# A list scheduler that issues products on part of the array in runs of one shape

## The chip, the core and the metric

The kernel runs on one core of one Trainium2 chip, in one launch. The metric is the time on the device in microseconds, median of the runs. TensorE (PE in the profile) multiplies; VectorE (DVE), ScalarE (ACT) and GpSimd (POOL) do the rest; the DMAs are issued from SyncE's queue (SP). PEld is the weight load that comes with each matmul.

## What is computed

Two transformer blocks of two layers each, on 256 tokens of width 1024, in float32. Cut to the parts that the change touches:

```python
def first_block(x, c, ...):                      # DEPTH = 2 layers
    for l in range(DEPTH):
        mod = c_act @ ada_w[l] + ada_b[l]        # adaLN vector, 6 x 1024
        h = rms_norm(x, norm1_g[l]) * (1.0 + sc1) + sh1
        proj = h @ w_in[l]
        y_a = diff_attention(...)                # 4 heads, two softmaxes of width 64 each
        y_b = gated_deltanet(...)                # chunks of 64 tokens, both directions
        merged = g_a * (y_a @ w_branch_a[l]) + g_b * (y_b @ w_branch_b[l])
        x = x + gt1 * (merged @ w_out[l])
        h = rms_norm(x, norm2_g[l]) * (1.0 + sc2) + sh2
        x = x + gt2 * (jnp.square(jax.nn.relu(h @ w_mlp1[l])) @ w_mlp2[l])

def diff_attention(...):
    s = jnp.einsum('bhtqd,bhtkd->bhtqk', qi, k) * scale      # contraction over 64
    p = jax.nn.softmax(s, axis=-1)
    a = p[:, :, 0] - lam * p[:, :, 1]

def gated_delta_rule_chunked(q, k, v, g, beta):  # per head and chunk of 64
    L = jnp.where(strict, jnp.einsum('bhncd,bhnmd->bhncm', kb, k) * decay, 0.0)
    T = lax.linalg.triangular_solve(eye + L, eye, ...)       # 64 x 64
    def step(state, inp):                                    # the scan over chunks
        v_new = u_i - w_i @ state
        o_i = qd_i @ state + qk_i @ v_new
        state = state * gl_i + kd_i.T @ v_new
```

The second block has two layers too: an attention stage of three kinds of heads, then 16 experts with 32 slots each, whose weights are 192 units of 1 MB a layer.

## The kernel before

Nothing in the kernel is issued as it is written. The program is recorded first: every operation becomes an `Op` with its engine, its operands and a cost in ns (`Plan.add`, `Plan.cost`), and a list schedule (`Plan.schedule`, line 465) then makes the order in which all engines' instructions are issued. Each engine takes, among the operations whose operands are there at the earliest time at which it could go on, the one with the largest `key`, the longest way to the end. `Plan.keys` works the keys out by a schedule that runs backwards. Operations get slots of tiles as they are scheduled; `can` says from when an operation's tiles have slots. `flush` (line 579) then issues all in the order of the plan's start times, which is why nearly every row of the profile has line 596.

What PE is given is of two kinds. **Full products** use 128 rows and 128 columns of the array: the projections (`dense`, lines 780 to 813), whose fp32 operands are split into two fp32r parts, three products for one, mostly 256 columns wide, and transposes. **Partial products** use part of the array. In block 1 the main ones are: the scores of the differential attention (`first` in `diffattn`, line 1493: 64 rows, in the upper and the lower half of the array by turns), the products of 64x64 blocks that complete the triangular inverse (`prod` in `deltanet`, line 1321: two corners of the array), and the products of the scan (lines 1399, 1403 and 1417: 128 rows by 64 columns, and 64 by 128). Further ones are 32 columns wide: column sums (line 1083), adaLN (lines 923 and 949), and the gates' weights of the recurrence (line 1116); the k k^T blocks (line 1216) have 128 by 64. In block 2 the attention has some of both kinds, and the experts' products are 128x32 (lines 2079 and 2095) and 32x128 (line 2102). Partial products that lie in different parts of the array and in one bank are recorded as one operation of two or four products (`add`, line 378).

The order on PE has one rule beyond the keys. `small` (line 518) counts up by the cost of each partial product whose contraction or whose width is 64 or less, and down by three times the cost of each other product; while it stands above `SMALL`, 1000 ns, other products are preferred (lines 533 and 534). Otherwise keys alone decide, so a partial product that has the larger key and a full one that has the next can stand in turns.

In block 1 `deltanet`, with the recurrence's chain of products and of steps on DVE, ACT and GpSimd, is woven with `fill` (line 1626): the attention, the gates' products and the first branch product. Weights come as units of 1 MB through a stream (`Stream`, line 740): ACT and DVE or GpSimd split each. In layer 0 the stream also brings 40 units of adaLN weights, with sums on DVE (line 942) and GpSimd (line 935).

Scratch tiles of 256 columns are of the kind `w1`: 8 in one pool and `W1X` = 6 more, in block 1 alone (line 1678).

Of the kernel before, what the change touches and what calls it, by code (L numbers as in the profile page):

```python
# [20 lines left out]
NEG = -1e30  # L21
# [8 lines left out]
W1X, NT = 6, 10  # L30


# ---------------------------------------------------------------- host layout
def _units(w, n=2):
    """[K, N] -> [N/(128 n), 128 (k in chunk), n, K/128, 128]: lhsT units of n column chunks."""
    k, c = w.shape
    a = w.reshape(k // 128, 128, c // (128 * n), n, 128).transpose(2, 1, 3, 0, 4)
    return np.ascontiguousarray(a).reshape(c // (128 * n), 128, -1)


def _rows(w, kc):
    """[K, N] -> [K/(128 kc), 128, kc, N]: rhs units of kc row chunks."""
    k, c = w.shape
    a = w.reshape(k // (128 * kc), kc, 128, c).transpose(0, 2, 1, 3)
    return np.ascontiguousarray(a).reshape(k // (128 * kc), 128, -1)


def _cols(v):
    """[n*128] -> [128, n]"""
# [14 lines left out]
def _shape_consts():  # L64
    """constants of the program, packed by the time that they are needed: c0 always, c1 and c2 per block"""
# [71 lines left out]
def _bias(rpb):  # L137
    """[4, 15, 31] -> [4, 128 (q in tile), 2 * 256]: bias of q over k, NEG outside q's window"""
# [92 lines left out]
def _rows_n(w, n):  # L231
    """[1024, N] -> [N/n, 128, 8, n]"""
# [5 lines left out]
# ---------------------------------------------------------------- order of issue  # L238


class Ref:
    """an access pattern of a tile that gets its place when its operations are issued"""
# [28 lines left out]

class Tile:
# [3 lines left out]
class Op:  # L276
    __slots__ = ("eng", "calls", "group", "outs", "dur", "dma", "deps", "succ", "tiles", "start", "end", "key", "what", "small")


class Plan:  # L280
    """Operations are recorded in program order and issued in the order of a list schedule: each engine takes,
    among the operations whose operands are there, the one with the longest way to the end. Costs and latencies
    are the guide's, in ns; they depend on shapes alone. A tile's slot is given out ahead of program order only if
    program order could still go on from there. Products that fill half of the array or less are not issued in long
    rows while others are ready: the array's clock falls when it is used little."""
# [4 lines left out]
    SMALL = 1000.0  # L290
# [12 lines left out]
    # -------------------------------------------------------- recording  # L303
# [22 lines left out]
    def box(r):  # L326
        """(what, partitions from, to, columns from, to)"""
# [37 lines left out]
    def add(self, eng, name, fn, args, kw):  # L365
# [4 lines left out]
        if eng == "P" and self.cols(ins[0]) < 128 and name == "matmul":  # L370
            p = self.ops[-1]
            rng = outs[0].ap.ap[0][1], outs[0].ap.offset // outs[0].ap.ap[0][0]
            if p.group and p.outs[0].t is outs[0].t and rng not in p.group:
                p.group.append(rng)
                self.access(p, n - 1, ins, outs)
                p.calls.append((fn, args, kw))
# [7 lines left out]
        if eng == "P":  # L384
            k, n_ = ins[0].shape[0], self.cols(ins[1])
            o.small = name == "matmul" and min(k, n_) <= 64
        o.eng, o.calls, o.dma, o.deps, o.succ, o.start, o.tiles = eng, [(fn, args, kw)], None, set(), [], None, []
# [38 lines left out]
    # -------------------------------------------------------- scheduling  # L426
# [3 lines left out]
    def keys(self, n0):  # L430
        """time to the end by a list schedule that runs backwards, in which every engine is single"""
# [33 lines left out]
    def schedule(self, slots):  # L465
        """slots: per kind of tile, the time at which each slot gets free"""
# [24 lines left out]
        def fit(e, t, dur):  # L491
            """the first time from t on at which engine e is idle for dur"""
# [8 lines left out]
        def can(i, t):  # L501
            """the earliest time from t on at which operation i's tiles have slots"""
# [15 lines left out]
        order, small = [], 0  # L518
        while len(order) < n - n0:
# [3 lines left out]
            for e, q in ready.items():  # L523
# [6 lines left out]
                if c:  # L530
                    t0 = min(c)[0] + 1
                    c = [(-ops[i].key, t, i) for t, i in c if t <= t0]
                    if e == "P" and small > self.SMALL:
                        c = [z for z in c if not ops[z[2]].small] or c
# [6 lines left out]
            if o.eng == "P":  # L541
                small = max(0.0, small + (o.dur if o.small else -3 * o.dur))
# [36 lines left out]
    def flush(self, place, slots, issue):  # L579
        """schedules what has been recorded, into what waits and has gaps; place(kind, slot): the slot's memory"""  # L580
# [8 lines left out]
        for i, place in self.waiting:  # L589
# [5 lines left out]
            for fn, args, kw in o.calls:  # L595
                self.tc.keep_in_program_order(fn(*map(real, args), **{k: real(v) for k, v in kw.items()}))  # L596
# [3 lines left out]
# ---------------------------------------------------------------- program  # L600


def _build(nc, tc, A, out):
# [10 lines left out]
    def sigm(o, x):  # L614
        """o = sigmoid(x) = exp(-log(1 + exp(-x))): the functions of a single table set"""
# [27 lines left out]
    with es:  # L643
# [10 lines left out]
        def issue(blocks, own, acc, quarters=(), last=False):  # L654
            """blocks: kind -> the blocks that its slots lie in; own: kind -> the pools of its further slots;
            acc: PSUM banks for accumulators; quarters: pools of the blocks whose quarters are tiles for themselves"""
# [66 lines left out]
        class FM:  # L723
            """feature-major activations: chunk pairs of 2 x 256 tokens, one tile each"""
# [15 lines left out]
        class Stream:  # L740
            """weights in the order of their use: loads run ahead, the split into two fp32r halves a little less"""
# [15 lines left out]
            def split(self, key):  # L757
                """loads and splits the next unit, if it isn't there yet"""
# [16 lines left out]
            def take(self, key):  # L775
                """an item that is used as it is"""
# [3 lines left out]
        def dense(st, key, n, kc, xhi, xlo, evac, fresh=False):  # L780
            """feature-major [128, 256] outputs, two per bank; a half of a unit at a time.
            n units of n * 2048 / (128 kc) column chunks; fresh: x comes in chunk by chunk"""
# [1359 lines left out]
```

## Time and profile before

| | us |
|---|---|
| median of 3 runs | 2407.26 (2403.64 to 2407.43) |
| span of the profiled execution | 2408.3 |
| PE busy | 1984.8 (82%) |
| DVE busy | 1159.4 (48%) |
| ACT busy | 786.9 (33%) |
| GpSimd busy | 465.6 (19%) |

The profile gives no time of its own for the profiled execution beside its span; the span is 1.0 us over the median of the runs. Block 1 takes about the first 1215 us, its two layers about 690 and 525; the first layer of block 2 ends about 1816 us. The views read are the busy times of chosen stretches, with the granted clock of PE (1.00 is 2.4 GHz, 0.50 is 1.2 GHz) and the DMA engines' share; the list of who waited for whom in a stretch; the timeline of PE, in which equal instructions that follow each other are one row; and the list of groups of instructions. A matmul's duration in the timeline overlaps with its neighbours', so what one costs is read from the starts. A product of fp32 operands stands as two instructions, one of fp32r as one.

### The profile page before, as it was taken

To read this page: it belongs to the slowest core of one execution; us is meant where nothing else is said; L and a number is where in the kernel's file an instruction comes from. 1 tells how busy PE (TensorE), PEld (TensorE's weight loads), DVE (VectorE), ACT (ScalarE), POOL (GpSimd) and SP (SyncE) were. 2 spreads that over 40 slices of the span, in tenths; PEclk is the share of its full clock that TensorE was granted. 3 is DMA by queue.
4 is the path that set the end of the run, shared out by engine and by line. 5 is a ranking of instruction groups with operands and counts; after the bars stand their busy time and mean duration, and the time that the engine had idled before them with its cause. 6 is when DMAs were issued, how large, how long until landed. Compare 5 with 4: busy or idle time off the path is not lost. (4 is left out here: it accounts for less than half of the span.)

```text
span 2408.3 us, 38449 instructions
## 1 busy us (share of the span) xinstructions
PE 1984.8 (82%) x16200; PEld 1437.7 (60%) x16200; DVE 1159.4 (48%) x1908; ACT 786.9 (33%) x1508; POOL 465.6 (19%) x278
## 2 busy tenths in 40 slices
PE   8688987778989999999999887666769988666665
PEld 5677777777987777999986542222237644222222
DVE  5998478999789623775557410000006731000001
ACT  4363343433457323654456210000015521000001
POOL 1555354455133312000020210000002111000000
PEclk7897898788999768999999888887779988877777
DMA  8354224566633310645544699999995579999997
GB/s 315 124 188 128 105 106 158 210 229 254 237 121 132 116 36 18 247 158 178 203 153 167 274 420 420 421 421 420 421 420 212 209 281 420 420 421 420 420 421 313
DMA packets 108253, 622.36 MB, mean 258 GB/s; under 512 B 27184, under 2 KB 28464, under 8 KB 34992
## 3 DMA queue, kind: packets, MB, share of 16 engines
q1 hardware_dynamic: 108080, 619.90, 65.4%
q8 instruction: 127, 2.08, 0.3%
q14 instruction: 46, 0.38, 0.0%
HBM read 617.24 MB, written 2.62 MB: 257 GB/s over the span
## 5 line engine op out<-in xcount | busy, mean ns | idle before, releaser
L596 PE MATMUL ps<-quarter,block 128*128 128x256 f32 (+1 forms) x5760 | 868.4, 304 | 72.5 <-DVE quarter L596 23.6
L596 PEld LDWEIGHTS ps<-quarter,block 128*128 128x128 f32 x5760 | 786.2, 205 | 114.9 <-issue 28.2
L596 PE MATMUL ps<-block,block 128*32 128x256 f32 (+4 forms) x5204 | 546.5, 431 | 137.9 <-DMA block<-in_w_up_dram 95.1
L596 PEld LDWEIGHTS ps<-block,block 128*32 128x32 f32 (+2 forms) x5204 | 274.4, 136 | 354.7 <-DMA block<-in_w_up_dram 159.3
L596 DVE TENSOR_TENSOR block<-block,block 128x1024 fp32r<-128x1024 f32 (+2 forms) x262 | 364.7, 1398 | 130.6 <-PE ps L596 73.1
L596 ACT ACTIVATE block<-block 128x1024 fp32r<-128x1024 f32 (+2 forms) x312 | 319.1, 1028 | 321.9 <-PE ps L596 292.8
L596 ACT ACTIVATE w<-ps 128x256 f32<-128x256 f32 (+1 forms) x138 | 52.3, 382 | 819.0 <-PE ps L596 818.9
L596 DVE TENSOR_TENSOR w<-w,ps 128x256 f32<-128x256 f32 x64 | 26.9, 421 | 544.3 <-ACT w L596 537.8
L596 POOL TENSOR_TENSOR block<-block,block 128x1024 fp32r<-128x1024 f32 x46 | 117.0, 2551 | 794.3 <-ACT block L596 387.8
L596 PE MATMUL ps<-block,w 128*32 128x256 f32 x2048 | 176.0, 500 | 25.8 <-ACT w L596 13.3
L596 PE MATMUL ps<-quarter,quarter 64*64 64x64 f32 (+6 forms) x1312 | 166.8, 304 | 6.9 <-DVE quarter L596 6.9
L596 PEld LDWEIGHTS ps<-block,w 128*32 128x32 f32 x2048 | 76.9, 142 | 116.2 <-issue 49.8
L596 PEld LDWEIGHTS ps<-quarter,quarter 64*64 64x64 f32 (+3 forms) x1312 | 113.2, 177 | 53.2 <-issue 20.0
L596 ACT ACTIVATE quarter<-quarter 128x512 f32<-128x512 f32 (+2 forms) x188 | 116.2, 628 | 85.0 <-DVE quarter L596 82.5
L596 ACT ACTIVATE quarter<-ps 128x512 f32<-128x512 f32 (+1 forms) x136 | 79.5, 592 | 151.2 <-PE ps L596 133.8
L596 DVE SCALAR_TENSOR_TENSOR w<-block,cT,w 128x256 f32<-128x256 f32 x140 | 126.5, 903 | 2.2
L596 DVE TENSOR_SCALAR w<-c,slot 128x256 f32<-128x256 f32 x32 | 12.5, 411 | 234.9 <-PE ps L596 234.8
L596 PE MATMUL ps<-w,w 32*128 32x256 f32 x512 | 106.7, 418 | 15.4 <-ACT w L596 15.1
L596 POOL TENSOR_TENSOR block<-block,cT 128x2048 f32<-128x2048 f32 x20 | 76.5, 3825 | 136.8 <-DVE w L596 41.0
L596 PEld LDWEIGHTS ps<-w,w 32*128 32x128 f32 x512 | 55.5, 185 | 69.2 <-issue 35.4
L596 DVE TENSOR_TENSOR quarter<-quarter,ps 128x512 f32<-128x512 f32 (+1 forms) x80 | 49.0, 629 | 84.7 <-PE ps L596 80.0
L596 POOL TENSOR_TENSOR block<-block 128x1024 f32<-128x1024 f32 (+1 forms) x40 | 85.2, 2131 | 2.4
(169 smaller groups left out, 1604.8 us busy)
## 6 DMA issues: line engine op xcount, KB each, us to landing
block<-in_w_gate_dram SPq DMA_DIRECT2D x144, 1024.0 KB, 19.8
block<-in_w_up_dram SPq DMA_DIRECT2D x128, 1024.0 KB, 19.8
block<-in_w_down_dram SPq DMA_DIRECT2D x128, 1024.0 KB, 19.8
block<-in_w_m_dram SPq DMA_DIRECT2D x64, 1024.0 KB, 4.8
block<-in_ada_dram SPq DMA_DIRECT2D x40, 1024.0 KB, 6.1
block<-in_w_dn_dram SPq DMA_DIRECT2D x16, 1024.0 KB, 4.8
block<-in_w_o_dram SPq DMA_DIRECT2D x16, 1024.0 KB, 7.0
block<-in_w_in_dram SPq DMA_DIRECT2D x12, 1024.0 KB, 12.1
```

What stands on the lines that cost most here:

```text
L596: self.tc.keep_in_program_order(fn(*map(real, args), **{k: real(v) for k, v in kw.items()}))
```

## The change

The rule with `small` goes. In its place, once PE has been given a partial product, it is given further operations of the same shape (rows and columns of the array) as long as one is among the candidates of that moment; a transpose counts as full. After a full product keys alone decide, as before. And whenever the shape changes while PE has been idle for less than `CHANGE` = 300 ns, the operation's start in the plan is set to 300 ns after the end of the one before. `W1X` falls from 6 to 3, so block 1 has 11 scratch tiles of 256 columns in place of 14. The further lines keep, for each operation, the source line that it comes from, and add no instruction. Cut to this:

```diff
-W1X, NT = 6, 10
+W1X, NT = 3, 10
...
-    SMALL = 1000.0
+    CHANGE = 300.0
...
-            o.small = name == "matmul" and min(k, n_) <= 64
+            o.shape = (k, self.cols(ins[0])) if name == "matmul" else (128, 128)
...
-        order, small = [], 0
+        order, shape = [], (128, 128)
...
-                    if e == "P" and small > self.SMALL:
-                        c = [z for z in c if not ops[z[2]].small] or c
+                    if e == "P" and shape != (128, 128):
+                        c = [z for z in c if ops[z[2]].shape == shape] or c
...
             if o.eng == "P":
-                small = max(0.0, small + (o.dur if o.small else -3 * o.dur))
+                if o.shape != shape and at["P"] > t - self.CHANGE:
+                    t = at["P"] + self.CHANGE
+                shape = o.shape
...
-            for fn, args, kw in o.calls:
-                self.tc.keep_in_program_order(fn(*map(real, args), **{k: real(v) for k, v in kw.items()}))
+            for fn, args, kw, n in o.calls:
+                self.tc.keep_in_program_order(
+                    call_at(n)(fn, tuple(map(real, args)), {k: real(v) for k, v in kw.items()}))
```

What this does to the order is seen at two places on PE. The first is in layer 1 of block 1, where the scores of a head begin. Before (all rows have line 596; `quarter` and `block` are tiles, `ps` a bank of PSUM, and 128x256 the output; rows that read a `block` are full products of the gates, the others are scores):

```order
L596 MATMUL ps_63<-quarter_1_5970,block_491 128x256
L596 MATMUL ps_91<-quarter_0_7254,quarter_3_7121 128x256
L596 MATMUL ps_63<-quarter_0_5976,block_491 128x256
L596 MATMUL ps_91<-quarter_3_7264,quarter_3_7121 128x256
L596 MATMUL ps_63<-quarter_1_5970,block_491 128x256
L596 MATMUL ps_91<-quarter_0_7254,quarter_0_7126 128x256
```

After (L838 is a full product, L1518 a score):

```order
L838 MATMUL ps_63<-quarter_1_6009,block_486 128x256
L1518 MATMUL ps_83<-quarter_0_7253,quarter_0_7167 128x256
L1518 MATMUL ps_91<-quarter_0_7253,quarter_0_7167 128x256
L1518 MATMUL ps_83<-quarter_2_7267,quarter_0_7167 128x256
L1518 MATMUL ps_91<-quarter_2_7267,quarter_0_7167 128x256
L1518 MATMUL ps_83<-quarter_0_7253,quarter_1_7176 128x256
L1518 MATMUL ps_91<-quarter_0_7253,quarter_1_7176 128x256
```

Scores and full products stood in turns, twelve times for a head; now 24 scores follow each other, those of the upper and the lower half of the array by turns.

The second is a little further on, in the 64x64 products of the triangular inverse (each row two products). Before:

```order
L596 MATMUL ps_79<-quarter_2_7431,quarter_0_6877 64x64 x2
L596 MATMUL ps_71<-quarter_3_5990,block_518 128x256
L596 MATMUL ps_79<-quarter_2_7431,quarter_0_6877 64x64 x2
L596 MATMUL ps_91<-quarter_0_7439,quarter_3_6888 64x64 x2
L596 MATMUL ps_67<-quarter_1_6006,block_491 128x256
```

After (L1346 is a 64x64 product, L836 a full one):

```order
L1346 MATMUL ps_83<-quarter_0_7336,quarter_2_6800 64x64 x2
L836 MATMUL ps_63<-quarter_1_5979,block_478 128x256
L1346 MATMUL ps_83<-quarter_0_7336,quarter_2_6800 64x64 x2
L1346 MATMUL ps_79<-quarter_1_7410,quarter_2_7345 64x64 x2
L1346 MATMUL ps_83<-quarter_0_7336,quarter_2_6800 64x64 x2
L1346 MATMUL ps_79<-quarter_1_7410,quarter_2_7345 64x64 x2
```

Between two full products stand eight such rows now, sixteen products, where one or two rows stood for most of the way. In between, one full product still comes: it has the largest key once no product of the shape is left.

## Rows read from the trace of the kernel before

**Rows 1.** Busy us and instructions by stretch, granted clock, DMA share; the first row names columns.

```profile
core 0: us, PE busy (x) PEld busy (x) DVE busy (x) ACT busy (x) POOL busy (x), PEclk, DMA share, GB/s
200.00:360.00 160.00, 143.09 (x1077) 113.57 (x1075) 107.92 (x171) 61.12 (x135) 70.52 (x50) 0.85 0.31 109
360.00:690.00 330.00, 270.75 (x2008) 257.96 (x2009) 291.42 (x353) 129.68 (x194) 131.64 (x57) 0.89 0.56 211
...
800.00:960.00 160.00, 154.95 (x918) 114.80 (x919) 61.61 (x125) 48.34 (x96) 31.16 (x31) 0.72 0.14 43
960.00:1215.00 255.00, 250.95 (x2045) 248.31 (x2044) 167.39 (x228) 132.02 (x196) 10.94 (x6) 0.99 0.55 197
1215.00:1340.00 125.00, 121.71 (x712) 95.84 (x711) 88.48 (x197) 76.73 (x184) 21.79 (x14) 1.00 0.44 162
1340.00:1816.00 476.00, 340.72 (x3525) 153.36 (x3524) 43.68 (x114) 52.55 (x127) 26.94 (x18) 0.81 0.98 407
...
1950.00:2383.00 433.00, 313.77 (x3332) 136.13 (x3330) 24.08 (x59) 35.39 (x85) 10.27 (x4) 0.81 0.99 412
```

**Rows 2.** Waits from 800 to 960 us: us in total, times, longest.

```profile
POOL quarter L596 <- PE ps L596: 72.3, 5, 48.4
DVE quarter L596 <- PE ps L596: 60.1, 18, 13.6
ACT quarter L596 <- PE ps L596: 57.3, 16, 17.7
```

**Rows 3.** Timeline of PE, layer 1, scores at full clock: start us, us, instruction.

```profile
813.39 0.38 PE L596 MATMUL ps<-quarter,quarter 64*128 64x256 f32 x1
813.70 0.39 PE L596 MATMUL ps<-quarter,block 128*128 128x256 f32 x1
814.02 0.38 PE L596 MATMUL ps<-quarter,quarter 64*128 64x256 f32 x1
```

**Rows 4.** Timeline of PE, layer 1, the same at half clock, and full products.

```profile
821.43 0.58 PE L596 MATMUL ps<-quarter,quarter 64*128 64x256 f32 x1
...
822.45 0.58 PE L596 MATMUL ps<-quarter,quarter 64*128 64x256 f32 x1
...
832.74 2.98 PE L596 MATMUL ps<-quarter,block 128*128 128x256 f32 x13
835.64 0.58 PE L596 MATMUL ps<-quarter,quarter 64*128 64x256 f32 x1
```

**Rows 5.** Timeline of PE, 64x64 products in turns, full and half clock.

```profile
235.41 0.33 PE L596 MATMUL ps<-quarter,quarter 64*64 64x64 f32 x4
...
235.98 0.33 PE L596 MATMUL ps<-quarter,quarter 64*64 64x64 f32 x4
...
858.39 0.48 PE L596 MATMUL ps<-quarter,quarter 64*64 64x64 f32 x4
...
859.31 0.48 PE L596 MATMUL ps<-quarter,quarter 64*64 64x64 f32 x4
```

**Rows 6.** Timeline of PE, layer 0, runs of scores and of 64x64 products.

```profile
213.68 0.86 PE L596 MATMUL ps<-quarter,quarter 64*128 64x256 f32 x10
214.47 1.33 PE L596 MATMUL ps<-quarter,block 128*128 128x256 f32 x9
...
238.64 0.91 PE L596 MATMUL ps<-quarter,quarter 64*64 64x64 f32 x24
239.49 0.39 PE L596 MATMUL ps<-quarter,block 128*128 128x256 f32 x1
```

**Rows 7.** As rows 1, for 4 us amid layer 1's turns.

```profile
836.00:840.00 4.00, 4.00 (x9) 2.28 (x8) 0.00 (x0) 0.00 (x0) 0.00 (x0) 0.50 0.46 195
```

**Rows 8.** Waits from 360 to 690 us.

```profile
PE ps L596 <- DVE quarter L596: 20.7, 8, 9.0
```

**Rows 9.** Groups of DVE from 360 to 690 us: count, busy us, mean ns.

```profile
L596 DVE SCALAR_TENSOR_TENSOR w<-block,cT,w 128x256 f32<-128x256 f32 x91 | 84.7, 930 | 1.7
```

More of the change, by code (lines that the diff above doesn't have):

```diff
@@ L1 @@
 import math
+import sys
 from bisect import bisect
@@ L269, in real, with line, call_at @@
         return x
+HELPERS = {"act", "tt", "ts", "stt", "mm", "sigm", "<lambda>"}
+CALLS = {}
+def line():
+    f = sys._getframe(2)
+    while f.f_code.co_name in HELPERS:
+        f = f.f_back
+    return f.f_lineno
+def call_at(n):
+    if n not in CALLS:
+        space = {}
+        exec(compile("\n" * (n - 1) + "def call(fn, a, k): return fn(*a, **k)", __file__, "exec"), space)
+        CALLS[n] = space["call"]
+    return CALLS[n]
 class Tile:
@@ L276 @@
 class Op:
-    __slots__ = ("eng", "calls", "group", "outs", "dur", "dma", "deps", "succ", "tiles", "start", "end", "key", "what", "small")
+    __slots__ = ("eng", "calls", "group", "outs", "dur", "dma", "deps", "succ", "tiles", "start", "end", "key", "what", "shape")
 class Plan:
@@ L375, in add @@
                 self.access(p, n - 1, ins, outs)
-                p.calls.append((fn, args, kw))
+                p.calls.append((fn, args, kw, line()))
                 if len(p.group) == 2:
@@ L385, in add @@
             k, n_ = ins[0].shape[0], self.cols(ins[1])
-            o.small = name == "matmul" and min(k, n_) <= 64
-        o.eng, o.calls, o.dma, o.deps, o.succ, o.start, o.tiles = eng, [(fn, args, kw)], None, set(), [], None, []
+            o.shape = (k, self.cols(ins[0])) if name == "matmul" else (128, 128)
+        o.eng, o.calls, o.dma, o.deps, o.succ, o.start, o.tiles = eng, [(fn, args, kw, line())], None, set(), [], None, []
         if eng == "S":
```

## The prediction, before the changed kernel had run

> **What bounds the kernel now.** I read the busy times by stretch first [rows 1]. The program falls into block 1 (two layers, up to about 1215 us) and block 2 (two layers, each with a stage of attention and a stage of experts). In the expert stages (1340 to 1816 us, and the like from 1950 on) the DMA engines are busy 0.98 of the time and PE 341 of 476 us: they last as long as their weights take, whatever PE's order. So what the change is worth is decided in block 1, and a little in the attention stages of block 2, and whatever is won there moves the expert stages forward whole.
>
> In block 1 the partial products stand in two stretches: 200 to 360 us (layer 0) and 800 to 960 us (layer 1), where the delta rule and the differential attention run, woven with the full products of the gates. The second is the clear one: PE is busy 155 of 160 us, DVE 62, ACT 48, the DMA engines 0.14 [rows 1], and the longest waits of DVE, ACT and GpSimd are all for PE: 60, 57 and 72 us [rows 2]. Yet PE issues only 918 instructions there, where it issues 2045 in the 255 us behind it; per 160 us that is 918 against 1283. Two things slow it: the alternation itself, and a granted clock of 0.72 against 0.99.
>
> The alternation is read off the starts in the timeline. At full clock (2.4 GHz) a full product and one 64-row product of the attention's scores take 0.63 us together (813.39 to 814.02) [rows 3]. The same pair takes 1.02 us at half clock (821.43 to 822.45) [rows 4]. With 64x64 products (two products, four instructions, and a full one) a turn is 0.57 us at full clock and 0.92 us at half [rows 5]. In runs the same work is cheap: ten score products take 0.79 us (0.08 each), 24 instructions of 64x64 0.85 us (0.14 for four) [rows 6], and full products among themselves 0.12 us each (255 us for 2045 instructions, nearly all full, in [rows 1]). At half clock a full one in a run takes 2.90 us / 13 = 0.22 [rows 4].
>
> The clock fell there without any wait: from 836 to 840 us PE is busy 4.00 of 4 us, in turns, at 0.50 [rows 7].
>
> In layer 0's stretch PE is busy 143 of 160 us and DVE 108, and behind it, from 360 to 690 us, DVE is busy 291 of 330 us [rows 1], with PE waiting for it [rows 8]. A gain of PE's in layer 0 therefore partly ends in a wait for DVE.
>
> **The change part by part.** *Fewer turns.* In the built order, PE goes from a full to a partial shape 318 times in block 1 before and 147 times after. In layer 1's stretch it is 123 before and 32 after: scores 44 to 3, 64x64 products 48 to 16, the scan's products (64x128 and 128x64) 31 to 13. In layer 0 it is 98 and 23: 32 to 6, 46 to 9, 20 to 8. The other 97 of block 1 become 92. No product is added or removed.
>
> *Price of a turn saved.* Scores, at full clock: 0.63 less what stays, 0.12 + 0.08, is 0.43 us. 64x64: 0.57 - 0.12 - 0.14 = 0.31 us. For the scan I take 0.31 too, the shape it is nearest to. At half clock, with the clock staying there: scores 1.02 - 0.22 - 0.14 = 0.66, the others 0.92 - 0.22 - 0.25 = 0.45 (what stays of the partial ones stretched by the ratio of the full ones, about 1.8).
>
> *Layer 1.* At full clock 41 x 0.43 + 32 x 0.31 + 18 x 0.31 = 33 us. A mean clock of 0.72 is half clock for 56% of the time; as a turn is 1.6 times as long then, some 44% of the turns. At half-clock prices the 91 turns are 27 + 14 + 8 = 49 us. Mixed: 0.56 x 33 + 0.44 x 49 = 40 us. PE waits for nothing in the stretch but 5 us at its start, and DVE, ACT and GpSimd wait for PE, so I count all of it on the path.
>
> *The clock.* Of 160 us, 40 go and 5 are the wait at the start, so some 115 us of PE work remain. If the clock stays at 0.72, nothing more comes. If it comes back to 0.85, as in layer 0's stretch with fewer turns per time, half clock falls from 56 to 30% of it: 30 us of work run at 0.12 in place of 0.22 per full product, which gives 14 us. Full clock throughout would give 29. I take 14. Runs of 64x64 fill little of the array too, so I don't take more.
>
> The Trainium skill (TensorE: Matmul & The Clock Gate, "Why this matters for your kernels") lays the loss of the clock to idle gaps between bursts of matmuls. The rows above show it lost with no gap. By that rule taking away the turns brings no clock back, and the sum would be 14 us less.
>
> *Waits that appear.* Full products now stand on average about seven places further back and the partial ones up to a hundred further forward, so less filler lies between the steps of the delta rule, each of which goes through ACT or DVE. PE's idle time in layer 0's stretch, with the same products, is 160 - 143 = 17 us; that is the bound. I take 4. Layer 1 in sum: 40 + 14 - 4 = **50 us**, between 40 - 17 = 23 and 40 + 29 = 69.
>
> *Layer 0.* 26 x 0.43 + 37 x 0.31 + 12 x 0.31 = 26 us at full clock. Here DVE's work (splits of weights and the adaLN sums) comes at the pace of the weight stream, which PE sets, so DVE gets its work earlier when PE is faster; but at the end of the stretch about 80 full products more are still to do than before, and their weights' splits lie in the stage in which DVE is the bound. I take half, **13 us**, between 0 (all of it ends in waits for DVE) and 35 (all, and a third more from the clock).
>
> *Attention of block 2.* Full to partial 29 to 16 times in each layer; 13 x 0.43 x 2 = 11 us at the price of scores. PE is busy 122 of 125 us there, DVE 88, clock 1.00 [rows 1]. I take **5 us**, between 0 and 11.
>
> *Experts.* Changes between partial shapes fall by about half there (162 to 85 and 177 to 94, every change counted). PE has 135 us to spare in the first of them, DMA is the bound: nothing. That cover would be gone only if PE's work there grew by those 135 us.
>
> *Three scratch tiles fewer* (11 in place of 14, of 256 columns, in block 1). They hold the squares, the rsqrt's intermediates and the adaLN's partial sums. No row shows a wait for such a tile. From 360 to 690 us DVE runs 91 adaLN steps of 0.93 us [rows 9], 13 units of seven; a slip of one such step for every second unit would be 6 us. A gain is excluded, as a slot less only takes a choice away. I take **2 us lost**, between 0 and 8.
>
> *The charge of 300 ns* for a change of shape makes the planner put PE's later operations, and so everybody's, at other times. DVE's order moves by five places on average. No row has a price for it; I take 0 and let the range carry 5 us either way.
>
> Sum: 50 + 13 + 5 - 2 = 66 us off the profiled span of 2408.3, so 2342.3. The median of the runs is 1.0 us under that span, so **2341 us**.
>
> **The rivals.** *The clock doesn't come back* (the half clock hangs on something other than the turns; it is what the Trainium skill's rule on idle gaps, in TensorE: Matmul & The Clock Gate, would make of it). Then the term of 14 falls out and the sum is 52: 2355. Against it speaks that 960 to 1215 us, with no turns, has 0.99, and the stretch just before, with 123, 0.72; for it, that in block 2's attention 29 turns go with a clock of 1.00 [rows 1].
>
> *The chain takes PE's place.* With the filler gone, PE waits for ACT and DVE between the steps of the delta rule for as long as in layer 0 now (17 us), and layer 0's gain ends in DVE: 23 + 0 + 0 - 2 = 21, so 2386. For it speaks the DVE share of 0.88 from 360 to 690; against it, that others wait three times 57 us or more for PE in layer 1.
>
> *Slower: scratch tiles run short in layer 0.* An adaLN unit holds its tile until four units are summed; with 11 tiles, a unit would wait for the next sum. From 360 to 690 us DVE has 39 us to spare, so a wait beyond that lengthens the stage. At 8 us a unit, 13 units lose 104 us, less the 39 to spare, so 65, which is where it eats the whole gain; at 9 us each it loses 78, and the time is 2342 + 78 = 2420. Against it: the order of DVE hardly moves.
>
> *Nothing measurable*: layer 1's gain is real, but what it releases meets a later wait of the same size, 2407 within 5. There is no row with such a wait behind 960 us (PE is busy 251 of 255).
>
> *Everything at its upper end*: 69 + 35 + 11 = 115, so 2292.
>
> That the change doesn't do what it says is excluded by the order.
>
> **How the numbers follow.** Forecast (2300 to 2378) 0.60; clock not back, 0.12; chain, 0.13; all upper ends, 0.03; nothing, 0.04; slower, 0.08. Faster by over 0.2% (about what a measurement of this kernel can tell from no change) is 0.60 + 0.12 + 0.13 + 0.03 = 0.88, within 0.04, slower 0.08. The range leaves out the slower case, the upper end and most of the case of nothing: 2300 to 2392, its slow end being the chain's 2386 with the charge's 5 us on top.
>
> **What would show it.** Right: in layer 1's stretch of the changed kernel, score products as groups of ten and more in the timeline, the stretch down from 160 to about 110 us, its clock above 0.8, PE still without waits; in layer 0 some 13 us less and longer waits of PE for DVE; expert stages of the same length, only earlier. Wrong on the turns: the stretch is as long, with PE idle. Wrong on the clock: shorter by about 36 us at 0.72 still. Wrong on the scratch: DVE's idle time in front of its adaLN steps grows from 360 to 690 us.

## The result and the profile after

The changed kernel takes 2352.4 us (median of 4 runs, 2351.5 to 2352.6) beside 2405.5 us for the kernel before: a ratio of 0.9775, 95% interval 0.9759 to 0.9790. The gain is 53 us where 66 were forecast; the profiled span is 2350.9 us. Rows of after carry their own line numbers (L835 to L838 are the full products of the dense layers, L1518 the scores, L1346 the 64x64 products of the delta rule), where all rows of before carry the helper's line.

The windows of the profiled run of after answer [rows 1]; the stretches end at about the same places of the program (the first starts at 200 us in both kernels), one each for layer 0, the work behind it, layer 1, the rest of block 1, and block 2's attention and experts:

```profile
core 0: us, PE busy (x) PEld busy (x) DVE busy (x) ACT busy (x) POOL busy (x), PEclk, DMA share, GB/s
200.00:335.00 135.00, 109.91 (x1091) 100.34 (x1092) 94.18 (x152) 65.90 (x140) 65.54 (x48) 0.88 0.32 114
335.00:671.00 336.00, 273.45 (x2025) 259.22 (x2023) 299.69 (x353) 128.72 (x194) 139.99 (x59) 0.90 0.57 212
...
802.00:897.00 95.00, 84.08 (x895) 72.75 (x894) 55.88 (x100) 45.41 (x92) 31.66 (x31) 0.93 0.21 64
897.00:1160.00 263.00, 258.87 (x2099) 255.77 (x2098) 170.35 (x230) 135.37 (x201) 11.17 (x6) 0.99 0.55 195
1160.00:1284.00 124.00, 117.99 (x720) 96.46 (x720) 88.87 (x199) 77.59 (x186) 21.35 (x14) 1.00 0.44 162
1284.00:1760.00 476.00, 320.85 (x3520) 145.20 (x3517) 43.20 (x113) 51.70 (x126) 26.93 (x18) 0.76 0.98 408
```

Layer 1's stretch is down from 160 to 95 us; PE's busy time in it from 155 to 84 us, for 895 in place of 918 instructions, and the clock is up from 0.72 to 0.93. PE now waits 11 us there, where it waited 5. The expert stage is as long as before, 476 us; it only starts earlier.

Pieces of the timeline of PE in that stretch show the runs, and two waits (start us, us, instruction, count; in brackets the wait before it). They answer [rows 3 to 6]:

```profile
811.43 0.38 PE L1518 MATMUL ps<-quarter,quarter 64*128 64x256 f32 x2
812.06 1.57 PE L1518 MATMUL ps<-quarter,quarter 64*128 64x256 f32 x22 [0.25 <-POOL quarter L1102]
815.84 0.33 PE L1346 MATMUL ps<-quarter,quarter 64*64 64x64 f32 x4 [2.21 <-DVE quarter L1336]
...
816.68 0.38 PE L835 MATMUL ps<-quarter,block 128*128 128x256 f32 x1
817.00 0.33 PE L1346 MATMUL ps<-quarter,quarter 64*64 64x64 f32 x4
817.26 0.58 PE L836 MATMUL ps<-quarter,block 128*128 128x256 f32 x1
...
824.48 1.76 PE L1346 MATMUL ps<-quarter,quarter 64*64 64x64 f32 x28 [5.32 <-ACT quarter L1527]
...
837.86 1.42 PE L1346 MATMUL ps<-quarter,quarter 64*64 64x64 f32 x32
839.20 0.38 PE L835 MATMUL ps<-quarter,block 128*128 128x256 f32 x1
839.51 1.43 PE L1346 MATMUL ps<-quarter,quarter 64*64 64x64 f32 x32
```

Twenty-two score products take 1.57 us, where each had cost 0.43 us more in a turn with a full one at full clock. Short windows of the same stretch show when the clock stood at its lower level:

```profile
823.00:827.00 4.00, 2.52 (x35) 2.18 (x37) 3.97 (x9) 1.62 (x5) 2.67 (x4) 0.50 0.00 0
827.00:831.00 4.00, 4.00 (x66) 3.56 (x62) 0.57 (x3) 1.51 (x5) 0.00 (x0) 0.51 0.02 4
838.00:842.00 4.00, 3.88 (x74) 3.35 (x73) 1.61 (x6) 1.70 (x6) 0.00 (x0) 1.00 0.00 0
842.00:846.00 4.00, 4.00 (x36) 3.20 (x35) 1.50 (x3) 2.15 (x3) 0.00 (x0) 1.00 0.02 4
846.00:865.00 19.00, 18.66 (x159) 17.57 (x158) 9.03 (x22) 14.63 (x32) 3.63 (x4) 1.00 0.31 112
865.00:897.00 32.00, 29.67 (x279) 24.62 (x276) 16.90 (x30) 14.22 (x30) 9.33 (x12) 1.00 0.10 34
```

Half clock is left for some 14 us: full products take 0.38 us up to 816.7 and 0.58 from 817.3, in four turns behind a wait of 2.2 us; a wait of 5.3 us ends at 824.5, and the clock is back at 831. All the rest runs at 1.00, where the kernel before stood at 0.50 with PE busy without a gap [rows 7]. No other waits of PE are long. The waits from 802 to 897 us (us in total, times, longest), beside [rows 2]:

```profile
POOL block L796 <- ACT quarter L1393: 31.4, 1, 31.4
POOL quarter L1432 <- PE ps L1428: 18.8, 1, 18.8
ACT block L794 <- PE ps L836: 12.9, 4, 6.2
ACT quarter L1358 <- PE ps L1346: 12.1, 4, 7.6
ACT quarter L1527 <- DVE t L1523: 9.4, 2, 8.4
DVE t L1522 <- PE ps L1518: 8.6, 2, 8.1
...
PE ps L1346 <- ACT quarter L1527: 5.3, 1, 5.3
...
PE ps L1346 <- DVE quarter L1336: 2.2, 1, 2.2
```

The first wait ends with a step of the delta rule on DVE (L1336). The second is put down to the exponential of the attention's scores on ACT (L1527), which had itself waited 8.4 us for DVE (L1523); what the 64x64 product needed of it, perhaps a bank of PSUM, the trace doesn't name. DVE was late because the four instructions of L1336 stood ahead and took 6.6 us, beside work of GpSimd:

```profile
814.81 6.63 DVE L1336 TENSOR_TENSOR quarter<-w,c 128x512 f32<-128x512 f32 x4 [0.47 <-DMA w<-xd]
```

So the largest term went as forecast. Where the rest of the gain is, and is not, a comparison by place tells. I matched each product in the two traces with its place in the program; the table has the time (us) at which the first product of a step starts, or the last one ends. The third kernel is an experiment of the next section.

| place in the program | before | after | after, without the charge |
|---|---|---|---|
| layer 0: first k k^T product | 97.1 | 107.0 | 95.9 |
| layer 0: end of the scan | 345.5 | 318.3 | 309.2 |
| layer 1: first product of its norm | 674.3 | 655.4 | 647.6 |
| layer 1: first k k^T product | 726.2 | 721.5 | 700.0 |
| layer 1: first scores | 813.4 | 811.4 | 782.1 |
| layer 1: end of the scan | 960.6 | 897.3 | 887.1 |
| end of block 1 | 1214.8 | 1159.9 | 1144.6 |
| first expert product | 1361.1 | 1305.4 | 1285.9 |
| last expert product | 2385.1 | 2327.5 | 2304.4 |

After is 27 us ahead at the end of layer 0's scan, 19 at layer 1's norm, and 2 at layer 1's scores; the 58 us at the end are made behind that, nearly all in layer 1's stretch. That looks as if layer 0's gain were worth nothing: it could be waited away at DVE, the bound behind layer 0. It was my first theory (A in the expectations), and it fell.

One execution stands behind each column. The kernel without the charge and three of the next section have the same order on PE up to layer 1's head, and begin its norm between 638 and 648 us; so a lead of a few us there is no more than that spread. From the norm to the k k^T products executions of one order agree better (52.0 to 52.4 us).

### The profile page after: what moved, and what is told of

Its sections match the earlier page's. It is cut to its first block, busy times and chain, and to the rows that moved or that the text cites. A ratio compares the mean times of both kernels' runs of the same rounds, so it can differ in the third digit from the quotient of the medians.

```text
span 2350.9 us, 38515 instructions
## 1 busy us (share of the span) xinstructions
PE 1837.1 (78%) x16200; PEld 1372.9 (58%) x16200; DVE 1160.6 (49%) x1908; ACT 787.2 (33%) x1508; POOL 463.4 (20%) x278
## 5 line engine op out<-in xcount | busy, mean ns | idle before, releaser
L2104 PE MATMUL ps<-block,block 128*32 128x256 f32 x4096 | 350.0, 472 | 188.1 <-DMA block<-in_w_gate_dram 98.0
L835 PE MATMUL ps<-quarter,block 128*128 128x256 f32 x1856 | 475.1, 300 | 25.2 <-DVE x L1669 7.0
L836 PE MATMUL ps<-quarter,block 128*128 128x256 f32 x1856 | 474.3, 300 | 8.0 <-DVE quarter L1662 5.1
L838 PE MATMUL ps<-quarter,block 128*128 128x256 f32 x1856 | 435.6, 295 | 8.8 <-DVE block L796 8.8
L796 DVE TENSOR_TENSOR block<-block,block 128x1024 fp32r<-128x1024 f32 (+1 forms) x258 | 353.8, 1375 | 148.0 <-PE ps L838 61.7
L794 ACT ACTIVATE block<-block 128x1024 fp32r<-128x1024 f32 (+1 forms) x296 | 309.4, 1050 | 335.8 <-PE ps L836 222.3
L835 PEld LDWEIGHTS ps<-quarter,block 128*128 128x128 f32 x1856 | 340.2, 203 | 36.7 <-issue 12.5
L2104 PEld LDWEIGHTS ps<-block,block 128*32 128x32 f32 x4096 | 126.4, 127 | 387.1 <-DMA block<-in_w_up_dram 162.5
L838 PEld LDWEIGHTS ps<-quarter,block 128*128 128x128 f32 x1856 | 342.1, 198 | 14.9 <-DVE block L796 9.7
L836 PEld LDWEIGHTS ps<-quarter,block 128*128 128x128 f32 x1856 | 339.1, 202 | 16.0 <-DVE quarter L1662 6.1
L796 POOL TENSOR_TENSOR block<-block,block 128x1024 fp32r<-128x1024 f32 x38 | 96.3, 2540 | 777.7 <-DMA block<-in_w_in_dram 372.4
L2107 ACT ACTIVATE w<-ps 128x256 f32<-128x256 f32 x32 | 12.3, 384 | 529.1 <-PE ps L2104 522.6
L2120 PEld LDWEIGHTS ps<-block,w 128*32 128x32 f32 x2048 | 77.7, 143 | 112.1 <-issue 52.4
L967 DVE SCALAR_TENSOR_TENSOR w<-block,cT,w 128x256 f32<-128x256 f32 x140 | 124.2, 891 | 2.5
L2123 ACT ACTIVATE w<-ps 128x256 f32<-128x256 f32 x32 | 12.3, 383 | 182.9 <-PE ps L2120 182.9
L2112 PE MATMUL ps<-c,w 128*128 128x128 f32 x64 | 19.3, 392 | 57.4 <-DVE w L2109 57.4
L2127 PE MATMUL ps<-w,w 32*128 32x256 f32 x512 | 41.3, 401 | 16.8 <-ACT w L2123 16.8
```

Of the source, the lines that this page charges most:

```text
L794: act(hi, r[:, h * n:h * n + n])
L796: tt(lo, r[:, h * n:h * n + n], f(hi), OP.subtract, e[self.ns % len(e)])
L835: mm(o, hi[:, j, k], xhi(k), k == 0, False)
L836: mm(o, hi[:, j, k], xlo(k), False, False)
L838: mm(o, lo[:, j, k], xhi(k), False, k == kc - 1)
L967: stt(t, r[:, k], cT[:, k:k + 1], t, OP.mult, OP.add)
```

## The experiments

Each experiment is an edit of the changed kernel. The ratios are to the kernel before, with 95% intervals; the kernel before had medians of 2405 to 2410 us beside them.

**One layer at a time.** The shape rule and its charge for the products of one layer only; elsewhere the old rule. `layer` is set where each layer is recorded, 2 for block 2 (for layer 0 the condition reads the other way):

```diff
             o.shape = (k, self.cols(ins[0])) if name == "matmul" else (128, 128)
+            o.small = name == "matmul" and min(k, n_) <= 64
+            if self.layer > 0:
+                o.small = False
+            else:
+                o.shape = (128, 128)
```

> The new rule and its charge hold for the products of layer 1 of block 1 and for block 2 alone; layer 0's products are chosen by the old rule (with the eleven scratch tiles of the changed kernel). Theory A: the gain is made in layer 1's stretch, where TensorE was the bound, and what the rule gains in layer 0 is waited away before layer 1's scores begin. Then this kernel takes 2347 to 2358 us, as the changed one (2352), its TensorE turns between full and partial products in layer 0 stand at about 150 as before, and the stretch from layer 1's first scores to the end of its scan stays at about 86 us. Rival B: layer 0's runs carry 10 to 20 us of the gain. Then it takes 2362 to 2373 us.

> The mirror of it: the new rule and its charge hold in layer 0 of block 1 alone, the old rule in layer 1 and in block 2. Theory A: 2400 to 2410 us, as the kernel before, since layer 0's stretch ends earlier but layer 1's scores start at the same time. Rival B: 2385 to 2395 us. In both, layer 1's stretch from the first scores to the end of the scan is again about 147 us long, with the granted clock at 0.5 to 0.6.

Measured: layer 1 and block 2 alone 2369.9 us, ratio 0.9838 (0.9822 to 0.9855); layer 0 alone 2388.9 us, 0.9919 (0.9900 to 0.9938). That is 39 and 19 us by the ratios, together 58, where both at once give 53 to 54. Theory A is refuted: layer 0's gain does reach the end. In the kernel with layer 0 alone, layer 1's norm is 25 us ahead of before, its k k^T products 18, its scores 24; its stretch takes about 150 us, at a clock of 0.76 where 0.5 to 0.6 was expected. In the kernel with layer 1 alone, the norm starts as before (674.5 us), but the scores 9 us later (822.3). So what is lost ahead of layer 1's scores is no wait for DVE that layer 0's gain runs into; rule or charge lose it between layer 1's own norm and its scores, mostly in the head up to the k k^T products (61 us, 52 before).

**The old rule with eleven scratch tiles.**

```diff
-                    if e == "P" and shape != (128, 128):
-                        c = [z for z in c if ops[z[2]].shape == shape] or c
+                    if e == "P" and small > self.SMALL:
+                        c = [z for z in c if not ops[z[2]].small] or c
...
-                if o.shape != shape and at["P"] > t - self.CHANGE:
-                    t = at["P"] + self.CHANGE
-                shape = o.shape
+                small = max(0.0, small + (o.dur if o.small else -3 * o.dur))
```

> The old rule without charge, and one change of the new kernel alone: eleven scratch tiles in place of fourteen. Theory A with free scratch tiles: 2400 to 2410 us, no difference from before. Rival C: the three tiles are missed in layer 0 and hide what the rule gains there; then 2412 us or more, and the rule with fourteen tiles would be worth that much more.

Measured: 2411.2 us, ratio 1.0012 (0.9996 to 1.0028). The three scratch tiles cost nothing that shows. The trace of after agrees: VectorE's adaLN steps wait as little as in [rows 9] (group of DVE from 335 to 671 us: count, busy us, mean ns, idle before):

```profile
L967 DVE SCALAR_TENSOR_TENSOR w<-block,cT,w 128x256 f32<-128x256 f32 x98 | 86.1, 883 | 1.7
```

**The rule without the charge.**

```diff
-    CHANGE = 300.0
+    CHANGE = 0.0
```

> The new rule with the charge for a change of shape set to nothing: block 1 has 187 turns from a full to a partial product in place of 143, by the built order. Theory A with turns that cost 0.4 us each where TensorE is the bound: layer 1 has 28 turns more, 10 us at most, so 2352 to 2364 us. Rival D: the charge only makes the planner's picture wrong (layer 0's first products stand 10 to 16 us later in the changed kernel); then this one is faster than it by 5 to 10 us, 2342 to 2347.

Measured: 2323.6 us, ratio 0.9632 (0.9613 to 0.9650). It is 29 us faster than the changed kernel by the medians and 34 by the ratios, and no kernel tried is faster beyond the noise; the charge costs as much as the rule gains in layer 0. Rival D had the sign and at most a third of the size. In the table, the lead of this kernel over after grows to 11 us by the first k k^T products of layer 0, stays at 8 to 9 up to layer 1's norm, grows to 22 at layer 1's k k^T products and to 29 at its scores. Then 19 us are lost, since without the charge layer 1's scores alternate more (26 changes from full to partial by the built order, 3 with it), and 13 more are won behind it.

From here theory E: the charge does its harm in the heads of the layers, by the order that the planner makes there, and would be of use in the stretches of scores alone.

**The charge with the old rule.**

```diff
-                    if e == "P" and shape != (128, 128):
-                        c = [z for z in c if ops[z[2]].shape == shape] or c
+                    if e == "P" and small > self.SMALL:
+                        c = [z for z in c if not ops[z[2]].small] or c
```

> The old rule (no run of more than 1 us of small products), with the charge of 300 ns for each change of shape: the charge by itself, without the preference for the same shape. The built order has 280 turns in block 1 as against 298 before, 45 of layer 0's 29 + 46 in scores and 64x64 products, 73 of layer 1's 89. Theory E: the charge alone does harm, 10 to 30 us slower than before: 2420 to 2440 us, with layer 1's k k^T products late. Rival H: the charge alone finds the runs and the rule adds little: 2380 us or less.

Measured: 2459.2 us, ratio 1.0202 (1.0168 to 1.0236): slower than before by 49 us, beyond what theory E asked for. Layer 1's norm is 29 us later than before, its first k k^T product 43, its first scores 51. The harm is done ahead of layer 1's stretch; the stretch itself (864 to 992 us) is 20 us shorter than before.

**The charge only where the partial products are many.**

```diff
                 kk, qk = pk
+                plan.charge = True
...
                 kd = [None] * 2
+                plan.charge = False
...
-                if o.shape != shape and at["P"] > t - self.CHANGE:
+                if o.charge and o.shape != shape and at["P"] > t - self.CHANGE:
```

(In the second kernel, `plan.charge = l == 1`.)

> The new rule everywhere; the charge of 300 ns only for products recorded between the k k^T products and the scan of each layer, where the rows of partial products are; elsewhere a change of shape is free for the planner. Theory E: the charge is worth having where turns are many and TensorE is the bound (it keeps layer 1's scores in 8 turns by the built order, 26 without it), and does harm in the head of the layers, where it puts TensorE late in the planner's picture and lets VectorE take other work first. Then layer 1's scores start near 785 us as without the charge (782), the stretch to the end of the scan takes 86 to 95 us (105 without, 86 with the charge everywhere), and the time is 2305 to 2318 us, below the kernel without charge (2324). Rival F: the charge moves VectorE's work in the stretch too and what it saves in turns is lost again: 2322 us or more. Rival G: layer 1's start is not set by the charge in its head: scores start after 800 us and the time is 2340 to 2352.

> As the kernel with the charge in both layers' stretches of scores, but in layer 1's alone; layer 0 is ordered as without the charge. Layer 0 has 93 turns by the built order as against 79 with the charge there. Theory E: the turns saved in layer 0 are worth 0.2 to 0.4 us each, so this kernel is 0 to 6 us slower than the one with both, 2306 to 2322 us. Rival F: the charge harms VectorE's order in layer 0, and this kernel is the faster of the two by 3 us or more.

Measured: 2327.8 us, 0.9649 (0.9619 to 0.9679), and 2326.0 us, 0.9654 (0.9617 to 0.9690); neither differs from the kernel without charge. Half of theory E holds: with no charge in its head, layer 1's scores start early (785.8 and 775.8 us). The other half falls, as rival F has it. The stretch of 101 us with the charge and of 105 us without it, as windows of the two profiles (with the charge first):

```profile
786.00:887.00 101.00, 86.74 (x845) 71.66 (x844) 56.92 (x104) 41.68 (x87) 27.84 (x29) 0.90 0.19 58
```

```profile
782.00:887.00 105.00, 101.41 (x848) 79.50 (x849) 55.59 (x108) 43.26 (x89) 28.07 (x29) 0.85 0.18 56
```

The charge takes 15 us off PE's work, by fewer turns and more full clock, and 11 of them come back as idle time of PE (14 us in place of 4). Nearly all of it is one wait of 11.3 us for the step L1336 (L1339 in that kernel) of the delta rule on DVE, which had itself waited 5.2 us for a DMA: the chain of the delta rule is the bound there once the turns are gone. The pair differs by 2 us, less than the runs of either spread, so whether layer 0's stretch gains from the charge stays open.

**Half the charge.**

```diff
-    CHANGE = 300.0
+    CHANGE = 150.0
```

> The new rule with a charge of 150 ns in place of 300. Theory E: the harm in the heads goes with the size of the charge, so the time lies between the kernel without charge (2324) and the one with 300 ns (2352): 2328 to 2348 us. Rival G: the order in the heads flips with any charge at all; then it is as late as with 300 ns, 2350 us or more, since layer 1 has 104 turns here as against 66.

Measured: 2365.8 us, ratio 0.9800 (0.9767 to 0.9834); slower than with 300 ns, not between. Rival G has the number and, with more turns, part of the reason; but the head of layer 1 doesn't flip, it does lie between (57 us from its norm to its k k^T products; 52 without charge, 66 with 300 ns). But the stretch takes 116 us, with 49 turns of 64x64 products, counted in the traces, where the neighbours have 16 (300 ns) and 26 (none), at a clock of 0.71:

```profile
799.00:915.00 116.00, 110.55 (x820) 84.72 (x820) 47.09 (x87) 40.29 (x84) 25.27 (x27) 0.71 0.14 42
```

The order doesn't follow the charge step by step; a little later start of one operation deals the whole stretch anew.

**The charge in layer 1's head alone.**

```diff
                 vv = vview(l)
+                plan.charge = l == 1
                 hh, hl = nx.finish()
...
                 kk, qk = pk
+                plan.charge = False
```

> The new rule everywhere; the charge of 300 ns in one place alone, the head of layer 1 of block 1, from the products of its first projections to its k k^T products; elsewhere a change of shape is free for the planner. The order up to layer 1's head is that of the kernel without charge, instruction for instruction; in the head the same instructions of VectorE, GpSimd and TensorE stand in another order. Theory E: here is a large part of what the charge costs: from the first products of layer 1's norm to the first k k^T product it takes 60 to 66 us as with the charge everywhere (66), not 52 as without it, and the time is 2334 to 2346 us as against 2324 without charge. Rival J: the harm is spread over the layers, or made in layer 0: this place gives under 5 us, 2320 to 2329 us.

Measured: 2346.8 us, ratio 0.9759 (0.9743 to 0.9776), 23 us above the kernel without charge by the medians; rival J falls, and the time stands just above theory E's 2346. From the norm's first product to the first k k^T product it takes 62 us in place of 52 (643.0 to 705.1), as theory E has it. But that is 10 of the 23: the stretch behind adds 14 us, 119 in place of 105, as it too is dealt anew, with 49 turns of 64x64 products in place of 26. In the changed kernel that stretch is 19 us shorter instead, so that 23 comes near the 29 is in part chance.

```profile
789.00:908.00 119.00, 110.79 (x883) 86.81 (x881) 54.02 (x100) 45.31 (x91) 25.53 (x28) 0.81 0.16 50
```

What happens in the head is looked for on DVE. The same piece of the program, from about the end of the norm's first products to the first k k^T product, in after and in the kernel without charge (windows, columns as above):

```profile
661.00:721.00 60.00, 44.77 (x305) 41.37 (x304) 53.19 (x96) 29.13 (x54) 19.97 (x10) 0.83 0.30 106
```

```profile
652.00:700.00 48.00, 40.40 (x298) 37.56 (x296) 43.38 (x95) 25.09 (x52) 14.03 (x8) 0.93 0.25 88
```

DVE is busy nine tenths of the time in both, so I take it that it sets the pace; with the charge it is busy 10 us more for one instruction more. The timelines of DVE and of GpSimd (POOL) in after show how:

```profile
665.57 2.35 DVE L869 TENSOR_TENSOR w<-w,w 128x256 f32<-128x256 f32 x1 [0.38 <-issue]
667.96 2.52 DVE L870 TENSOR_TENSOR w<-w,w 128x256 f32<-128x256 f32 x1
...
694.39 3.49 DVE L1262 TENSOR_TENSOR quarter<-c,t 128x512 fp32r<-128x512 f32 x2
697.81 2.06 DVE L796 TENSOR_TENSOR block<-block,block 128x1024 fp32r<-128x1024 f32 x1
699.79 3.53 DVE L1205 TENSOR_SCALAR quarter<-quarter,v 128x256 f32<-128x256 f32 x2
```

```profile
665.26 2.38 POOL L796 TENSOR_TENSOR block<-block,block 128x1024 fp32r<-128x1024 f32 x1 [2.22 <-ACT block L794]
667.85 2.34 POOL L796 TENSOR_TENSOR block<-block,block 128x1024 fp32r<-128x1024 f32 x1 [0.22 <-ACT block L794]
...
700.74 2.44 POOL L796 TENSOR_TENSOR block<-block,block 128x1024 fp32r<-128x1024 f32 x1
```

And DVE at the same place without the charge, GpSimd idle beside it:

```profile
656.17 0.43 DVE L869 TENSOR_TENSOR w<-w,w 128x256 f32<-128x256 f32 x1 [1.05 <-ACT w L867]
656.63 0.42 DVE L870 TENSOR_TENSOR w<-w,w 128x256 f32<-128x256 f32 x1
```

The two instructions of L869 and L870 end just after GpSimd's do (2.35 and 2.52 us in place of 0.43 and 0.42), and so does the pair of L1205, behind GpSimd's third split. In the changed order GpSimd's splits of weights (L796) lie beside these steps of DVE, and DVE has one row product (L1262) and two splits more to do ahead of the k k^T products. It isn't one-sided: without the charge two small steps of the gates (L1167, L1169) last 2.4 and 2.3 us beside GpSimd. These two pairs nearly cancel: by the groups of the two windows the first takes 4.1 us more and the second 3.9 less, while the splits grow from 3.6 us for three to 6.9 for five and the row products from 0.7 us for one to 3.5 for two. And in the kernel with the charge in this head alone L869 and L870 take 0.42 us each, yet the head is 62 us long. So the pair shows how a step is held up, not why the head is longer. That the charge, put in this head alone, makes it 10 us longer is shown by that run; how much of that is the side-by-side and how much the work put ahead was not tried apart.

**The rule without charge, one layer at a time** (the two edits above together).

> The new rule without any charge, in layer 0 of block 1 alone; the old rule in layer 1 and in block 2. If the gains of the layers are two separate sums, this one gives what layer 1's norm shows in the kernel without charge, 22 to 32 us: 2376 to 2387 us. If layer 0's gain is waited away where layer 1 keeps the old rule, it is 2390 us or more.

> The new rule without any charge, in layer 1 of block 1 and in block 2 alone; the old rule in layer 0. Two separate sums: what is left of the 82 us that the kernel without charge gains, 50 to 60 us: 2347 to 2359 us. Layer 1's stretch from the first scores to the end of the scan is then 100 to 110 us long, with more turns than in the changed kernel, and its head takes 52 us. If the layers' gains overlap, it is 2335 us or less.

Measured: layer 0 alone 2380.0 us, 0.9894 (0.9876 to 0.9911); layer 1 and block 2 alone 2353.9 us, 0.9777 (0.9751 to 0.9804). That is 26 and 54 us off, 79 together, as against 82 (from the 2405.5 us of the result) to 89 (by the ratio) for both at once: near enough to two separate sums. In the first of them layer 1 keeps the old order and its old stretch, beside whose row those above stand:

```profile
782.00:929.00 147.00, 147.00 (x875) 107.05 (x875) 49.27 (x97) 43.21 (x89) 25.31 (x26) 0.72 0.13 40
```

## Why the prediction was right, and where its terms were off

**Direction, bound and place** were right: block 2's expert stages only moved forward, and layer 1's stretch carries the gain. By the table the 58 us are 19 up to layer 1's norm, less 14 in its head and 3 from there to the scores, 53 in its stretch and 3 in block 2.

**Layer 1 (forecast 50).** The stretch from the first scores to the end of the scan went from 147 to 86 us, 61 less; about 8 of these are full products that are done behind it instead (254 us before, 263 after, from there to the end of block 1), so 53. Inside the term two parts were off and cancel. I took 14 us for a clock of 0.85; at the measured 0.93, half clock for 14% of the time, the same sum gives 22, toward my upper 29. I took 4 us for new waits, bounded by 17, and PE waits 11 where it waited for nothing from the first scores on. 40 + 22 - 11 = 51. The 40 for the turns was not measured by itself.

**The clock.** The rival in which it doesn't come back fell: 0.72 to 0.93, with runs of small products and with more idle time of PE than before, not less (11 us for 5). The number of turns alone doesn't give the clock: counted in the traces, 68 turns from full to partial in the stretch without the charge stand beside 0.85, 67 with 150 ns beside 0.71. The rule of the Trainium skill that I set against it (TensorE: Matmul & The Clock Gate, "Why this matters for your kernels", on idle gaps) may describe the 14 us about the two waits that are left, which begin in turns as well; it doesn't describe the 0.50 at 4.00 us busy of 4 [rows 7].

**Layer 0 (forecast 13, bounds 0 to 35).** It is 19 us with the charge and 26 without, about the whole price of the turns (26 us at full clock for those of the changed kernel), where I took half. The step that failed is the halving, for waits that end in DVE. Without the charge the scan ends 36 us earlier, and 10 of these are given back up to layer 1's norm. The windows from the end of the scan to that norm show to what (before, after, without the charge):

```profile
345.00:674.00 329.00, 269.71 (x2022) 257.52 (x2021) 291.71 (x346) 128.80 (x201) 137.11 (x60) 0.89 0.56 211
```

```profile
318.00:655.00 337.00, 279.21 (x2087) 266.08 (x2087) 297.52 (x354) 131.86 (x208) 140.57 (x61) 0.90 0.57 213
```

```profile
309.00:647.00 338.00, 278.64 (x2068) 266.76 (x2067) 296.45 (x358) 133.24 (x214) 134.64 (x60) 0.88 0.57 212
```

PE's idle time is 59, 58 and 59 us, and its waits for DVE there are 47, 44 and 39 us in sum: not longer, where I had expected them longer. What is longer is PE's own work, 65 and 46 products more (9 us), which stood ahead of the scan's end before. Like the 8 us of layer 1 they are moved, not lost: 36 less 9 is 27. The clock from 195 us to the end of the scan rose as well, from 0.84 to 0.88; how much of the 27 is the clock was not tried apart.

**The charge (forecast 0, at most 5 either way)** is the term that was mis-sized: 29 us by the runs with and without it, and 49 us alone. I had written that no row has a price for it and that DVE's order moves by five places on average; a mean doesn't tell what a move costs where it falls. By the table it costs 11 us ahead of layer 0's k k^T products, 14 in layer 1's head, where DVE is 0.9 busy, and 8 from there to the scores, gives 19 back in the stretch, and costs 13 behind it. With the two apart, the rule is worth 82 us, where my terms for it came to 68, and the charge costs 29. Two errors of opposite sign left the time 11 us above the forecast; that it came so near is luck.

**Attention of block 2 (forecast 5).** In the first layer it is 146.3 us from the end of block 1 to the first expert product, then 145.5, and 141.3 without charge; in the second, between the expert products of the two layers, 165.1, 163.3 and 159.4. So the rule gives 11 us, my upper bound, and with the charge 3 are left. **Scratch tiles (2 lost):** nothing measurable. **Experts (0):** right.

## What to carry over

Where a row shows an engine busy all the time at half clock with alternating tile shapes, price the alternation from the starts of two neighbouring turns, at both clock levels: here the sum by that price came within 2 us of the measured one in layer 1. A cost put into a list scheduler is not free of charge even when it is near the truth (300 ns beside 0.31 to 0.43 us per turn): it moves every engine's order, so look for the stage in which another engine is about 0.9 busy, and try the choice rule and the cost apart; here the rule without the cost is the faster kernel, 2323.6 us.

## What the runs showed of the chip that I had not expected

VectorE and GpSimd can hold each other up for whole instructions: DVE's 128x256 products of two tiles took 2.35 and 2.52 us beside GpSimd splits of 2.4 us, and 0.42 us without one. The four instructions of L1336 took 6.6 us beside GpSimd in after, and 2.7 us in the kernel with the charge in both stretches, where GpSimd was idle. The adaLN steps of L967, 0.88 us in the mean, are two kinds: of the 98 from 335 to 671 us of after, 71 run without a GpSimd instruction beside them and take 0.48 us, 27 run beside one and take 1.94 us in the mean. The other way round, a GpSimd split took 6.5 us beside a row of DVE's instructions in the kernel with the charge in layer 1's head alone. The Trainium skill says this (SBUF — State Buffer, "Who interferes with whom": the port pair that the two share is locked for a whole instruction), and the rows agree; I had not read it into the change, since no GpSimd instruction is added by it.

The clock stood at 1.00 while PE ran 64x64 products in groups of 32 (838 to 842 us of after) and at 0.50 while it ran the same ones in turn with full products [rows 5]: the lower level went with the alternation, not with the small products as such. It didn't follow at once either way: a few turns ran at 1.00 (842 to 846 us), and groups of 32 at 0.50 behind a wait of 5.3 us, until the clock rose at 831 us.
